# Modulation vectors from turned-over weights, by one fused multiply and sum each, moved into the mixers

## The chip, the core and the metric

The kernel runs on one core of a Trainium2 chip. A core has TensorE (matrix products), VectorE (DVE), ScalarE (ACT), GpSimd (POOL) and SyncE (SP, which here issues nearly all transfers); they run side by side and wait for each other by semaphores. The metric is the device time of one execution in microseconds, lower is better.

## The reference, cut to what matters

A decoder trunk of two layers over x (512 positions by 1024 channels). Each layer has three sub-layers, SwiGLU, mixer, SwiGLU, and each of these is scaled and shifted by vectors that are computed from one conditioning vector c:

```python
cs = silu(c)                                             # (1, 1024)
mod = (cs @ ada_w[l] + ada_b[l]).reshape(1, 3, 3, 1024)  # ada_w[l]: 1024 x 9216
h = rmsnorm(x, norm_g[l, s]) * (1 + mod[s, 1]) + mod[s, 0]
x = x + (0.5 if s != 1 else 1) * mod[s, 2] * sublayer(h)
```

So there are 2 x 3 x 3 = 18 modulation vectors of 1024 elements, named (l, s, j) below: layer, sub-layer, and j = 0 shift, 1 scale, 2 gate. Each is a product of a vector of 1024 with a 1024 x 1024 block of `ada_w`, 4 MB of f32 weights.

## The kernel before, in words

Activations stay in SBUF turned over: `xT` holds 128 channels by 512 positions in each of 8 chunks. Every large product is done three times in fp32r with operands split in a high and a low part: `hi = cast(w)` on ACT, `lo = w - hi` on DVE (`Unit.split`, L214 and L215; `sub`, L146), then hi·xh, hi·xl, lo·xh on TensorE (`step`, L235 to L237). The SwiGLU halves (called FFN here) do most of their up projections by a seven-product scheme (`Sums`, `product`, `seven`, L585 and L558), which adds DVE work before each product. A sub-layer ends in `finish`, and `boundary` makes the next norm and the first products of the next sub-layer.

Work beside the main line is written as generators. `tick()` is called after every second `step` (six matmuls) and after each chunk in `values_turned` (twelve matmuls of 256 columns); it adds `rate * share` to a due count and runs one `next` of the current modulation generator for each whole unit. `share` is 0.5 in the up part of an FFN and 2.2 in its down part, and in a mixer the 2.2 of the FFN before it still holds. A gate that a `down` needs and that is not ready is finished there in one go (`while sub_layer not in ready`).

`modulation(l, s, j)` reads the 4 MB as 16 tiles of 128 x 512 (contraction on the partitions), four in flight (`AHEAD`). Each tile is multiplied by a per-partition scalar of `cs` and added to an accumulator on DVE (`weighted`, L309 and L311). After 8 tiles `partition_sums` adds over the partitions: DVE transpose (L316) and reduce (L318), four POOL copies (L322), a DVE reduce (L324), four POOL copies (L327). `modulation_end` adds the bias (L300), then for j = 1 also L303. One vector is 22 `next`s. Sixteen vectors are made so: four in the first FFN, two in the first mixer, four in the second FFN, three in the third, two in the second mixer, one in the last FFN.

The first two vectors, (0,0,1) and (0,0,0), are made in the opening. `ada_load(k)` brings the columns of chunk k, `prepare(k)` runs eight DVE multiply-adds of 128 x 256 (L1266, L311), one add (L1270), two small matmuls with `ones` (L1273), the ends, then t = xT * rms (L1278), hh and u on ACT (L1279, L1280), and hl on POOL (L1281). TensorE multiplies six units chunk by chunk (L1308). The rms of the first norm is a chain of POOL instructions for each of the four row blocks (`rstd_of`, L367 to L372).

F is a pool of 19 tiles of 128 x 512 f32 that all of this shares; a tile that is taken again has to wait for its last reader. Loads into F and into `raw` (four buffers for weights) go through the one SP queue in its order. The framework orders the instructions of each engine by its own estimate of when they are ready, near the order of the program but not equal to it; once ordered, an engine works in order.

In `up()` of an FFN, `begin(m)` starts the seven products of the pair m, m+1: it loads the weights of the pair and does the first product. In the first FFN of layer 0 three units m = 0, 1, 2 are already done in the opening (`first`), and `begin(2)` runs at m = 1 although unit 2 is in `first`; what it starts there is not used.

Of the kernel before, what the change touches and what calls it, by code (L numbers as in the profile page):

```python
# [30 lines left out]
P = 128  # L31
D = 1024
# [15 lines left out]
AHEAD = 4  # L48
CONV_STEPS = (4, 8)
RATE_FIRST, RATE_FFN, RATE_MIX = 0.8, 0.4, 0.2  # L50
# [66 lines left out]
def trunk(ctx: ExitStack, tc: tile.TileContext, x, c, ada_w, ada_b, norm_g, ffn_w_gate, ffn_w_up, ffn_w_down,  # L117
# [152 lines left out]
    vec = const.tile([P, 2 * 72 + 112], F32, name="vec")  # L270
    V_C, V_N, V_CW, V_F = 144, 152, 200, 248
# [24 lines left out]
    def modulation_end(l, s, j, dst, src, k):  # L296

        n = dst.shape[1]
        b = l * 72 + s * 24 + j * 8 + k
        V.tensor_tensor(dst, src, vec[:, b:b + n], op=ALU.add)  # L300
        if j == 1:
            g = V_N + l * 24 + s * 8 + k
            V.scalar_tensor_tensor(dst, dst, 1.0, vec[:, g:g + n], op0=ALU.add, op1=ALU.mult)  # L303
        elif j == 2 and s != 1:
            V.tensor_scalar(dst, dst, 0.5, None, op0=ALU.mult)

    def weighted(acc, w, k):
        if k == 0:
            V.tensor_scalar(acc, w, cs[:, 0:1], None, op0=ALU.mult)  # L309
        else:  # L310
            V.scalar_tensor_tensor(acc, w, cs[:, k:k + 1], acc, op0=ALU.mult, op1=ALU.add)  # L311

    def partition_sums(acc):

        flat = F.take()
        V.transpose(flat.ap, acc)  # L316
        part = sp.tile([P, 16], F32, tag="part", bufs=2, name="part")
        V.tensor_reduce(part, flat.ap.rearrange("p (j i) -> p j i", i=32), op=ALU.add, axis=AX.X)  # L318
        flat.give()
        four = sp.tile([32, 4, 16], F32, tag="four", bufs=2, name="four")  # L320
        for a in range(4):
            G.tensor_copy(four[:, a], part[32 * a:32 * a + 32])  # L322
        one = sp.tile([32, 16], F32, tag="one", bufs=2, name="one")
        V.tensor_reduce(one, four.rearrange("p a j -> p j a"), op=ALU.add, axis=AX.X)  # L324
        dot = sp.tile([P, 4], F32, tag="dot", bufs=2, name="dot")
        for a in range(4):
            G.tensor_copy(dot[32 * a:32 * a + 32], one.rearrange("p (k a) -> p a k", a=4)[:, a])  # L327
        return dot

    def modulation(l, s, j):  # L330

        m = mod(l, s, j)
        ahead = []

        def fetch(n):
            if n < 2 * NC:
                w = F.take()
                col = s * 3 * D + j * D + n // NC * S
                nc.sync.dma_start(w.ap, ada_w[l, n % NC * P:(n % NC + 1) * P, col:col + S])
                ahead.append(w)  # L340

        for n in range(AHEAD):
            fetch(n)
        for half in range(2):
            acc_slot = F.take()
            acc = acc_slot.ap
            for k in range(NC):
                w = ahead.pop(0)
                weighted(acc, w.ap, k)
                w.give()  # L350
                fetch(half * NC + k + AHEAD)
                yield
            yield
            dot = partition_sums(acc)
            acc_slot.give()
            yield
            modulation_end(l, s, j, m[:, 4 * half:4 * half + 4], dot, 4 * half)
            if half:
                ready.add((l, s, j))
            yield  # L360


    def rstd_of(st, n, eng=V):

        w = sp.tile([P, 4, 4], F32, tag="rs", bufs=3, name="rs")
        ms, q, e = (w[:, k, :n] for k in range(3))
        eng.tensor_scalar(ms, st, 1.0 / D, EPS, op0=ALU.mult, op1=ALU.add)  # L367
        G.tensor_tensor(q, ms, minus_half[:, :n], op=ALU.pow)
        G.tensor_tensor(e, q, q, op=ALU.mult)
        G.tensor_tensor(e, e, ms, op=ALU.mult)  # L370
        G.tensor_scalar(e, e, -0.5, 1.5, op0=ALU.mult, op1=ALU.add)
        G.tensor_tensor(q, q, e, op=ALU.mult)  # L372
        return q
# [271 lines left out]
    def ffn(l, i, get, first, whole):  # L645
# [45 lines left out]
        def up(part):  # L691
            modulating["share"] = SHARE_UP
            for m in range(*part):
                if m in acts:
                    continue
                if m < len(first) or m % 2:
# [8 lines left out]
                    if m % 2:  # L705
                        begin(m + 1)
# [484 lines left out]
    for r in range(2):  # L1191
        nc.sync.dma_start(xin[r].ap, x_rows[r])
    c_rows = rows([c.rearrange("b (k p) -> (b k) p", p=P), norm_g.rearrange("l s (k p) -> (l s k) p", p=P),
          conv_w.rearrange("l t (k p) -> (l t k) p", p=P), final_g.rearrange("(k p) -> k p", p=P)], V_C)
# [3 lines left out]
    cs = const.tile([P, NC], F32, name="cs")  # L1198
# [3 lines left out]
    def ada_load(k):  # L1202
        s = F.take(4)
        v = s.ap.rearrange("p (k m) -> p k m", k=NC)
        for j in range(2):
            col = (1 - j) * D + k * P
            nc.sync.dma_start(v[:, :, j * P:(j + 1) * P],
                              ada_w[0][:, col:col + P].rearrange("(k p) m -> p k m", p=P))
# [20 lines left out]
    q = []  # L1229
    for r in range(4):  # L1230
        A.activation(hl[:, 0:2].rearrange("p a b -> p (a b)"), xin[r].ap, AF.Square, accum_out=ssq[:, r:r + 1])
        q.append(rstd_of(ssq[:, r:r + 1], 1, G))
# [10 lines left out]
        if r == 1:  # L1243
            c_rows()
            A.activation(cs, vec[:, V_C:V_C + NC], AF.Silu)
            b_rows()
    rb = bank("at")
    for r in range(4):
        T.transpose(rb[:, r * P:(r + 1) * P], q[r].to_broadcast([P, P]), ident)
# [3 lines left out]
    ada_load(2)  # L1253
# [156 lines left out]
```

## Time and profile before

| | us |
|---|---|
| median of 3 runs (2702.79 to 2708.17) | 2703.82 |
| the profiled execution | 2702.54 |
| its span, first to last instruction | 2700.7 |
| PE busy | 2632.2 (97%) |
| DVE busy | 1898.2 (70%) |
| ACT busy | 1167.8 (43%) |
| POOL busy | 311.2 (12%) |
| DMA, mean over the span | 121 GB/s |

The mean granted TensorE clock is 0.991 of full speed. Busy time of PE is not PE at its peak, since matmuls overlap; what shows that PE waits is idle time between its instructions. The shares are means over stages that differ, so the rows below go by stage.

### The profile page before, as it was taken

What the parts mean: (1) busy time and instruction counts of PE and PEld (TensorE: products, weight loads), DVE (VectorE), ACT (ScalarE), POOL (GpSimd) and SP (SyncE); (2) the same over time, 40 slices, a digit from 0 to 9 for tenths busy, and PEclk for the clock granted to TensorE, in tenths of its full rate; (3) what the DMA queues carried; (4) which work ended last, traced back from release to release, by engine and by line L of the source; (5) the groups of instructions that cost most, each with busy time, mean ns of one, the idle gap of its engine ahead of it and who ended that gap; (6) DMA issues with size and microseconds to landing.
All of it is one profiled execution on the core that took longest, in us unless ns stands there. A gap on an engine that the chain in (4) does not pass through costs nothing.

```text
span 2700.7 us, 41538 instructions
## 1 busy us (share of the span) xinstructions
PE 2632.2 (97%) x16321; PEld 2357.8 (87%) x16321; DVE 1898.2 (70%) x2987; ACT 1167.8 (43%) x2202; POOL 311.2 (12%) x887
## 2 busy tenths in 40 slices
PE   6899999999999999999999999999999999999998
PEld 5788999888888889899998999988888888989998
DVE  7997878665463349997788987767646534787666
ACT  4433454443453235344554544543443423535443
POOL 3110103110010001100021000321110000200001
PEclk8999999999999999999999999999999999999999
DMA  8644435432222233563335541534322322342321
GB/s 251 222 158 149 131 123 161 129 94 82 82 82 91 86 117 108 189 198 100 109 107 192 171 127 61 180 110 137 98 56 87 124 75 90 106 129 89 115 69 73
DMA packets 320209, 328.08 MB, mean 121 GB/s; under 512 B 10130, under 2 KB 283917, under 8 KB 320013
## 3 DMA queue, kind: packets, MB, share of 16 engines
q1 hardware_dynamic: 319684, 325.29, 38.0%
q8 instruction: 128, 2.10, 0.3%
q14 instruction: 69, 0.56, 0.1%
q10 hardware_dynamic: 328, 0.13, 0.0%
HBM read 323.25 MB, written 2.13 MB: 120 GB/s over the span
## 4 chain that ended last, share of the span: by engine, by line
PE 76%; DVE 12%; ACT 4%; DMA 3%; issue 2%; POOL 2%; ACTq 0%; SPq 0%; DVEq 0%; POOLq 0%
PE mm L235 12%; PE mm L236 12%; PE mm L558 12%; PE mm L237 12%; PE o L558 6%; DVE slots_r L146 4%; PE mm L1073 3%; PE at L558 3%; PE o L235 2%; PE o L237 2%; PE o L236 2%; DVE slots_f L311 2%; DMA raw<-in_ffn_w_down_dram 2%; PE at L237 2%; PE at L235 2%
## 5 line engine op out<-in xcount | busy, mean ns | idle before, releaser
L215 DVE TENSOR_TENSOR slots_r<-raw,slots_r 128x512 fp32r<-128x512 f32 (+2 forms) x578 | 360.2, 641 | 299.4 <-PE mm L236 155.0
L214 ACT CAST slots_r<-raw 128x512 fp32r<-128x512 f32 (+1 forms) x584 | 323.4, 582 | 411.3 <-PE mm L237 157.3
L237 PE MATMUL mm<-hh,slots_r 128*128 128x512 f32 (+1 forms) x1320 | 482.8, 366 | 7.5 <-DVE slots_r L215 7.5
L235 PE MATMUL mm<-hh,slots_r 128*128 128x512 f32 (+1 forms) x1320 | 487.8, 370 | 0.0
L236 PE MATMUL mm<-hl,slots_r 128*128 128x512 f32 (+1 forms) x1320 | 483.5, 366 | 0.0
L146 DVE TENSOR_TENSOR slots_r<-raw,slots_r 128x1024 fp32r<-128x1024 f32 (+3 forms) x402 | 379.5, 969 | 90.2 <-ACT slots_r L549 32.6
L549 ACT CAST slots_r<-raw 128x1024 fp32r<-128x1024 f32 x274 | 283.4, 1048 | 351.6 <-DVE raw L585 146.9
L237 PEld LDWEIGHTS mm<-hh,slots_r 128*128 128x128 f32 x1320 | 248.8, 188 | 51.1 <-DVE slots_r L215 7.8
L235 PEld LDWEIGHTS mm<-hh,slots_r 128*128 128x128 f32 x1320 | 249.1, 189 | 36.9
L236 PEld LDWEIGHTS mm<-hl,slots_r 128*128 128x128 f32 x1320 | 249.2, 189 | 36.2
L558 PE MATMUL mm<-slots_r 128*128 128x256 f32 x1872 | 240.8, 284 | 6.9 <-ACT slots_r L549 5.8
L558 PE MATMUL mm<-hh,slots_r 128*128 128x256 f32 x1264 | 236.7, 283 | 9.1 <-ACT slots_f L581 6.6
L558 PE MATMUL o<-slots_r 128*128 128x256 f32 x1872 | 236.4, 284 | 5.2 <-DVE slots_r L146 3.1
L558 PEld LDWEIGHTS mm<-slots_r 128*128 128x128 f32 x1872 | 230.9, 192 | 9.8 <-ACT slots_r L549 6.8
L558 PEld LDWEIGHTS o<-slots_r 128*128 128x128 f32 x1872 | 229.9, 191 | 8.4 <-DVE slots_r L146 4.2
L236 PE MATMUL mm<-slots_r 128*128 128x512 f32 (+1 forms) x584 | 213.1, 365 | 1.2 <-DVE slots_r L146 1.2
L235 PE MATMUL mm<-slots_r 128*128 128x512 f32 (+1 forms) x584 | 212.7, 364 | 0.6 <-ACT slots_r L676 0.6
L237 PE MATMUL mm<-slots_r 128*128 128x512 f32 (+1 forms) x584 | 212.2, 363 | 0.0
L558 PEld LDWEIGHTS mm<-hh,slots_r 128*128 128x128 f32 x1264 | 199.1, 190 | 12.7 <-ACT slots_f L581 9.5
L311 DVE SCALAR_TENSOR_TENSOR slots_f<-slots_f,cs 128x512 f32<-128x512 f32 (+1 forms) x272 | 192.2, 721 | 12.0 <-DMA slots_f<-in_ada_w_dram 11.1
L585 DVE TENSOR_TENSOR raw<-raw 128x1024 f32<-128x1024 f32 x156 | 189.6, 1217 | 1.4
L558 PE MATMUL mm<-hl,slots_r 128*128 128x256 f32 x632 | 177.7, 281 | 0.0
(207 smaller groups left out, 4518.7 us busy)
## 6 DMA issues: line engine op xcount, KB each, us to landing
slots_f<-in_ada_w_dram SPq DMA_DIRECT2D x256, 256.0 KB, 2.9
raw<-in_w_in_dram SPq DMA_DIRECT2D x52, 1024.0 KB, 5.1
raw<-in_ffn_w_gate_dram SPq DMA_DIRECT2D x43, 1024.0 KB, 5.2
raw<-in_ffn_w_up_dram SPq DMA_DIRECT2D x43, 1024.0 KB, 5.3
raw<-in_ffn_w_down_dram SPq DMA_DIRECT2D x32, 768.0 KB, 5.8
raw<-in_w_in_dram SPq DMA_DIRECT2D x48, 512.0 KB, 5.2
raw<-in_ffn_w_down_dram SPq DMA_DIRECT2D x20, 512.0 KB, 3.6
slots_f<-in_ada_w_dram SPq DMA_DIRECT2D x16, 512.0 KB, 7.5
```

What stands on the lines that cost most here:

```text
L146: V.tensor_tensor(out_, a, b, op=ALU.subtract)
L214: A.copy(hv, src)
L215: (eng or V).tensor_tensor(lv, src, f(hv), op=ALU.subtract)
L235: T.matmul(dst, hi, xh[:, cols], start=first, stop=False)
L236: T.matmul(dst, hi, xl[:, cols], start=False, stop=False)
L237: T.matmul(dst, lo, xh[:, cols], start=False, stop=last)
L311: V.scalar_tensor_tensor(acc, w, cs[:, k:k + 1], acc, op0=ALU.mult, op1=ALU.add)
L549: A.copy(hv, src)
L558: T.matmul(dst, a, b, start=first and k == i == n == 0, stop=True, skip_group_check=True)
L585: V.tensor_tensor(dst, x, y, op=ALU.subtract)
L1073: T.matmul(dst, a, b, start=k == 0 and r % 2 == 0 and n == 0, stop=True, skip_group_check=True)
```

## The change

- The weights arrive turned over (`ada_t`: 9216 x 1024 for each layer), so the contraction runs along the free axis. `cs` becomes a tile of 128 x 1024, the vector repeated on all partitions by a transfer and Silu applied there; it holds two tiles of F to the end.
- `weighted` is one DVE instruction (`tensor_tensor_reduce`) over 128 x 1024 f32: multiply by `cs`, sum along the row, one output element on each partition. A vector takes 8 of them, 8 loads of 512 KB, one end, 9 `next`s. `partition_sums` goes.
- In the opening `prepare(k)` runs two of these in place of the nine instructions and the matmuls with `ones`; t of chunk 0 and all of hl move from POOL to DVE. The four rms chains become one over 4 columns, after the last row block.
- `rstd_of` keeps `pow` on POOL and does the rest on DVE, three instructions in place of four, also at every boundary.
- The FFNs make no modulation vectors but for three in the first one. The first mixer makes ten: (0,1,2), (0,2,1), (0,2,0), (0,2,2), three of (1,0,·), three of (1,1,·); the second mixer three. The rate there is 0.28 in place of 0.2, and one load is in flight (`depth=1`) in place of four.
- `begin(m + 1)` is not called where unit m + 1 is in `first`.

```diff
-AHEAD = 4
-RATE_FIRST, RATE_FFN, RATE_MIX = 0.8, 0.4, 0.2
+RATE_FIRST, RATE_FFN, RATE_MIX = 0.6, 0.3, 0.28
...
-    def weighted(acc, w, k):
-        if k == 0:
-            V.tensor_scalar(acc, w, cs[:, 0:1], None, op0=ALU.mult)
-        else:
-            V.scalar_tensor_tensor(acc, w, cs[:, k:k + 1], acc, op0=ALU.mult, op1=ALU.add)
+    def weighted(m, k, w):
+        V.tensor_tensor_reduce(out=w, in0=w, in1=cs.ap, scale=1.0, scalar=0.0, op0=ALU.mult, op1=ALU.add,
+                               accum_out=m[:, k:k + 1])
...
-    def modulation(l, s, j):
+    def modulation(l, s, j, depth=2):
         m = mod(l, s, j)
         ahead = []
-        def fetch(n):
-            if n < 2 * NC:
-                w = F.take()
+        def fetch(k):
+            if k < NC:
+                w = F.take(2)
+                nc.sync.dma_start(w.ap, ada_rows(l, s, j, k))
                 ahead.append(w)
+        for k in range(depth):
+            fetch(k)
+        for k in range(NC):
+            w = ahead.pop(0)
+            weighted(m, k, w.ap)
+            w.give()
+            fetch(k + depth)
             yield
+        modulation_end(l, s, j, slice(0, NC))
+        ready.add((l, s, j))
+        yield
...
         G.tensor_tensor(q, ms, minus_half[:, :n], op=ALU.pow)
-        G.tensor_tensor(e, q, q, op=ALU.mult)
-        G.tensor_tensor(e, e, ms, op=ALU.mult)
-        G.tensor_scalar(e, e, -0.5, 1.5, op0=ALU.mult, op1=ALU.add)
-        G.tensor_tensor(q, q, e, op=ALU.mult)
+        V.tensor_tensor(e, q, q, op=ALU.mult)
+        V.scalar_tensor_tensor(e, e, -0.5, ms, op0=ALU.mult, op1=ALU.mult)
+        V.scalar_tensor_tensor(q, e, 1.5, q, op0=ALU.add, op1=ALU.mult)
...
-                    if m % 2:
+                    if m % 2 and m + 1 >= len(first):
                         begin(m + 1)
...
+    cs = F.take(2)
+    nc.scalar.dma_start(cs.ap, c.to_broadcast([P, D]))
+    A.activation(cs.ap, cs.ap, AF.Silu)
...
+    q = rstd_of(ssq, 4)
...
     def prepare(k):
         s, v = ada_in.pop(k)
+        for j in range(2):
+            weighted(mod(0, 0, j), k, v[:, j])
+            modulation_end(0, 0, j, slice(k, k + 1))
         s.give()
         t, u = F.take(), F.take()
-        (V if k else G).tensor_tensor(t.ap, xT[:, k], rbs.ap, op=ALU.mult)
+        V.tensor_tensor(t.ap, xT[:, k], rbs.ap, op=ALU.mult)
...
-        G.tensor_tensor(hl[:, k], u.ap, f(hh[:, k]), op=ALU.subtract)
+        sub(hl[:, k], u.ap, f(hh[:, k]))
...
+        if l == 0:
+            modulate((RATE_FIRST, modulation(0, 0, 2)),
+                     *((RATE_FFN, g) for g in (modulation(0, 1, 1), modulation(0, 1, 0), bias_rows())))
+        else:
+            modulate()
...
+        ahead = [(l, 1, 2), (l, 2, 1), (l, 2, 0), (l, 2, 2)]
+        if l + 1 < DEPTH:
+            ahead += [(l + 1, s, j) for s in range(2) for j in (1, 0, 2)]
+        modulate(*((RATE_MIX, modulation(*a, depth=1)) for a in ahead if a not in ready))
```

## Rows read from the trace of the kernel before

**Rows 1.** Busy time by stretch: stretch, length, each engine, clock, DMA share, GB/s.
```profile
0.00:79.00 79.00, 54.73 (x218) 42.60 (x219) 58.41 (x123) 31.64 (x52) 30.35 (x47) 0.85 0.88 255
92.00:400.00 308.00, 302.45 (x2023) 277.31 (x2022) 263.73 (x371) 129.54 (x200) 29.22 (x70) 0.99 0.47 151
...
448.00:690.00 242.00, 241.29 (x1344) 208.37 (x1343) 151.43 (x269) 102.86 (x273) 42.59 (x182) 1.00 0.35 105
...
1042.00:1343.00 301.00, 291.84 (x2049) 272.92 (x2050) 263.14 (x351) 133.54 (x190) 20.79 (x64) 0.99 0.44 141
...
1400.00:1700.00 300.00, 296.86 (x2116) 279.13 (x2115) 256.05 (x332) 136.82 (x199) 14.04 (x48) 1.00 0.43 139
...
1760.00:1830.00 70.00, 70.00 (x442) 62.61 (x441) 45.59 (x81) 31.60 (x86) 14.33 (x64) 1.00 0.39 113
...
2350.00:2650.00 300.00, 295.01 (x2082) 276.49 (x2080) 227.42 (x276) 137.32 (x192) 3.70 (x16) 0.99 0.31 101
```

**Rows 2.** Busy time by stretches of 50 us, the same columns.
```profile
1100.00:1150.00 50.00, 46.80 (x285) 41.76 (x284) 47.53 (x70) 17.42 (x24) 4.87 (x19) 1.00 0.48 156
...
1500.00:1550.00 50.00, 50.00 (x398) 48.96 (x397) 46.55 (x63) 26.45 (x42) 2.86 (x8) 1.00 0.54 175
```

**Rows 3.** PE in order of time: start, us, line; idle before it and its releaser.
```profile
91.40 0.80 PE L237 MATMUL mm<-hh,slots_r 128*128 128x512 f32 x1 [7.55 <-DVE slots_r L215]
```

**Rows 4.** Groups of DVE instructions by form: busy us, mean ns, idle before.
```profile
L215 DVE TENSOR_TENSOR slots_r<-raw,slots_r 128x512 fp32r<-128x512 f32 x466 | 314.6, 689 | 277.0 <-PE mm L236 153.5 <-PE o L236 42.9 <-issue 33.0
L585 DVE TENSOR_TENSOR raw<-raw 128x1024 f32<-128x1024 f32 x156 | 189.6, 1217 | 1.4
L311 DVE SCALAR_TENSOR_TENSOR slots_f<-slots_f,cs 128x512 f32<-128x512 f32 x224 | 168.1, 755 | 12.0 <-DMA slots_f<-in_ada_w_dram 11.1
...
L316 DVE STREAM_TRANSPOSE slots_f<-slots_f 128x512 f32<-128x512 f32 x32 | 22.5, 703 | 0.1
...
L318 DVE TENSOR_REDUCE part<-slots_f 128x16 f32<-128x512 f32 x32 | 21.6, 676 | 0.2
...
L309 DVE TENSOR_SCALAR slots_f<-slots_f,cs 128x512 f32<-128x512 f32 x32 | 15.4, 480 | 0.9 <-DMA slots_f<-in_ada_w_dram 0.9
...
L300 DVE TENSOR_TENSOR mod<-dot,vec 128x4 f32<-128x4 f32 x32 | 5.2, 162 | 22.0 <-POOL dot L327 21.9
...
L1322 DVE TENSOR_TENSOR slots_f<-hh,hl 128x2048 f32<-128x2048 f32 x2 | 4.6, 2284 | 1.2 <-POOL hl L1281 1.2
```

**Rows 5.** DVE in order of time: the first instruction on weights of `ada_w`.
```profile
13.43 0.61 DVE L1266 TENSOR_SCALAR slots_f<-slots_f,cs 128x256 f32<-128x256 f32 x2 [2.99 <-DMA slots_f<-in_ada_w_dram]
```

**Rows 6.** ACT in order of time: the first and the last hh of the opening.
```profile
24.34 0.81 ACT L1279 ACTIVATE hh<-slots_f,mod,mod 128x512 fp32r<-128x512 f32 x1 [3.58 <-DVE mod L303]
...
73.55 0.82 ACT L1279 ACTIVATE hh<-slots_f,mod,mod 128x512 fp32r<-128x512 f32 x1 [5.24 <-DVE mod L303]
```

**Rows 7.** Busy time by stretch in the opening, columns as in the first group.
```profile
4.50:7.50 3.00, 2.37 (x11) 2.40 (x12) 0.69 (x1) 2.25 (x4) 0.19 (x1) 1.00 1.01 372
10.00:13.00 3.00, 1.54 (x7) 1.54 (x8) 0.44 (x1) 2.39 (x6) 1.82 (x9) 0.74 1.17 306
30.00:50.00 20.00, 13.73 (x52) 10.02 (x52) 17.61 (x40) 6.25 (x10) 5.92 (x4) 0.89 0.80 207
```

**Rows 8.** Groups of PE instructions from 78.9 to 81.7 us.
```profile
L558 PE MATMUL mm<-hh,slots_r 128*128 128x256 f32 x16 | 2.9, 276 | 0.0
L558 PE MATMUL mm<-hl,slots_r 128*128 128x256 f32 x8 | 2.2, 276 | 0.0
```

**Rows 9.** First mixer, matmuls of L237 alone: PE, PEld, clock, DMA share, GB/s.
```profile
448.00:690.00 242.00, 92.39 (x235) 44.06 (x234) 1.00 0.35 105
```

**Rows 10.** First mixer, matmuls of L1073 alone, the same columns.
```profile
448.00:690.00 242.00, 42.21 (x356) 42.05 (x357) 1.00 0.35 105
```

**Rows 11.** Who waited for the weights of `ada_w`: engine, tile, line: us, times.
```profile
  DVE slots_f L311: 11.1, 12
```

**Rows 12.** Transfers issued in the first 110 us: count, KB each, us to landing.
```profile
slots_f<-in_x_dram SPq DMA_DIRECT2D x4, 512.0 KB, 5.1
```

## The prediction before the run

> **What bounds the kernel now.** I read the busy time by stretch first, with cuts at the stages. TensorE is idle for next to nothing in the mixers: 0.7 us of 242 in the first one. It loses time in two kinds of place. The opening has 24.3 us of idle PE in 79, and its granted clock is at 0.85. The four FFNs have 5.5, 9.2, 3.1 and 5.0 us, 22.8 in all [rows 1]. The DVE column of the same rows is the reason to look at: 264 of 308, 263 of 301, 256 of 300 and 227 of 300 us in the FFNs against 151 of 242 in the mixer. The finer cut shows that the share alone does not fix the loss: at 47.5 of 50 us PE lost 3.2, at 46.6 of 50 nothing [rows 2]. The largest single gap stands right behind the opening: 7.55 us until a DVE split at 91.40 [rows 3]. So this kernel is bound by TensorE, and by DVE in the opening and in the FFNs. A change pays where it takes DVE work out of those, and costs where it puts it somewhere that becomes as full.
>
> **What a vector costs.** Now, on DVE: 14 multiply-adds of 0.755 us, 2 multiplies of 0.480 and for each half 0.703 + 0.676 + 0.162, together 14.6 us, and 22.0 us of waiting for POOL over 16 vectors, 1.4 each; 16 us [rows 4]. A few shorter instructions are left out. The fused instruction over 1024 elements is not in this trace. Its nearest row is the subtraction of two f32 tiles of 128 x 1024, 1.217 us; nothing speaks for less, since the 512-element form takes 0.689 and the time grows with the elements. Above, the bound is two passes, for which the 128 x 2048 row stands, 2.284 us. I take 1.25, by the near row and a little for writing the sum: a vector is then 8 x 1.25 + 2 x 0.16 = 10.3 us [rows 4].
>
> The multiply-add of today also reads two f32 tiles from SBUF (the weights and the accumulator) and takes 0.755 us for 512 elements, near the 0.689 of a plain two-tile operation and far from 1.2 [rows 4]. [...]
>
> **The opening.** Per chunk DVE gets 2 x 1.25 for the sums, three ends of 0.16, t and hl at 0.69 each: 4.36 us, 34.9 for eight chunks, and six splits of 0.69 stay on it: 39 us [rows 4]. The first weights are used at 13.43 [rows 5]; the repeated `cs` is 0.5 MB more, 1.4 us at 372 GB/s, and the weights come in long rows, as x does, at up to 372 in place of 306, 0.6 us less for the first MB [rows 7]: 14.2. Without gaps the last hh would come at 53; with DVE busy for 88% of the time, as it is from 30 to 50 us [rows 7], at 58.5. It comes at 73.55 now, 49.2 us behind the first one, 7.0 per chunk [rows 6]. The first hh no longer waits for four POOL chains and a product with `ones`, but eight chunks in series set the end and not the first one. That is 15 to 20 us, and I take 17. The lower bound is the transfer: x, `cs`, eight MB of `ada_w` and four MB of weights are 15.2 MB, which at the 255 GB/s of the whole opening [rows 1] land at 63, so that the last hh comes at 66: 7.5 us. The upper bound is 22, with less contention than now. POOL loses hl and most of the rms and gains nothing.
>
> What follows the last hh up to 91.40 is DVE work of the FFN that stays, so the 7.55 gap moves and does not shrink. The unused product is 24 matmuls in 2.7 us [rows 8], but they lie ahead of that gap; PE would have waited there. Its saving is the split of 1.2 us on DVE: 1 us.
>
> **The FFNs.** The first keeps three vectors of 10.3 in place of four of 16: 33 us less of 264. The second loses 64 us of DVE work, the third 48, the last 16, all of theirs. Some idle stays at the start of each, where the sums for the seven products fill DVE in any case. I keep 1.5 to 2 us each: gains of 4, 7, 1.5 and 3 of the idle in [rows 1], 15.5 in all. Bounds: 6, if the gaps hang on the sums, and 22, all idle.
>
> **The mixers** pay. Ticks in the first stretch: 235 / 2 + 356 / 12 = 147 in 242 us, one every 1.65 us [rows 9, 10]. Ten vectors are 90 `next`s at 0.28 x 2.2 = 0.616 a tick, 146 ticks, 240 us: the same stretch. Its DVE work is 151 us, some 25 of it the vectors of today; 126 + 103 = 229 of 242, 95% [rows 1]. The second mixer makes three in 44 ticks, 72 us: 46 - 11 + 31 = 66 of 70 [rows 1]. At such shares PE lost 0 to 3.2 us in 50 [rows 2], so 0 to 20 us over 314. I take 7, nearer the lower end, because in a mixer the splits run ahead of PE.
>
> **The waits added** are those of `pow` at every boundary: DVE starts it, POOL computes, DVE goes on. Behind the waiting instruction stand the residual updates, for which the norm and the next products wait. Three DVE instructions of 0.16 replace four POOL ones, and each side keeps its hand-overs; 0, within 2 either way. Fewer SP issues (128 in place of 256 for the 16 vectors) are worth nothing by themselves, since SP is not what PE waits for.
>
> **Sum** against the profiled execution of 2702.5 (span 2700.7 and 1.8 around it): -17 - 1 - 15.5 + 7 = -26.5, so 2676. The median of the runs lies 1.3 above that execution: 2677.
>
> **Rivals.**
>
> *The opening is held by its transfers.* It gains 7.5, and the FFNs keep the gaps of their first sums, so 9.5; the mixers cost 7. 2704 - 10 = 2694. For it: DMA is at 0.88 over the whole opening [rows 1]. Against: the mean includes waits for free tiles, and from 30 to 50 us DMA is less busy than DVE [rows 7].
>
> *The single load in flight takes the gain back.* This is the one on the slower side. With `depth=1` the next 512 KB are asked for when the sum before is queued, often into the tiles just freed, while up to eight logits and other tiles fill F. A load that starts only then holds DVE for its landing, 5.1 us [rows 12], and everything on SP's queue behind it, `raw` loads included. DVE has 13 us to spare in the first mixer. It decides when 13 + 33.5 us are used up, that is 46 / 5.1 = 9 of the 80 loads fully exposed; with 12, the time is 2704 + 15 = 2719. For it: F is short of pairs in the mixers and DVE is near full. Against: DVE waited only 12 times, 11.1 us in all, for 256 such loads [rows 11].
>
> *The fused sum runs at half rate*, 2.28 us [rows 4]. A vector costs 18.6: 126 + 186 = 312 us of DVE in 242, 70 over; 35 + 56 = 91 in 70, 21 over; the opening gains nothing; the FFNs 14. 2704 + 77 = 2781. [...]
>
> **How the numbers follow.** My forecast has 65%, its own range 2660 to 2692. Held transfers 18%, the single load 12%, the half rate 5%. A measurement of this kernel can tell about 0.2%, 5.4 us, from no change. Held transfers: 15 of the 18 lie below 2698.4, 3 within. The single load: 9 of 12 slower, 3 within. So faster 80%, same 6%, slower 14%. The range goes from 2656 (the opening at its bound of 22, the FFNs at 22, the mixers at 0, less a little) to 2704, which leaves out the slower cases and a few per cent below.
>
> **What would show it.** Right: the fused sum at 1.2 to 1.3 us; the last hh of the opening near 56 us and the long PE gap near 74; idle PE in the second FFN down to 2 us; DVE at 93% or more in the first 240 us of the first mixer, and PE idle there a few us more than 0.7. Wrong: a last hh later than 66 (transfers); DVE idle for `ada_t` in the mixers for more than 20 us, with PE gaps behind it (single load); a fused sum over 2 us; or FFNs whose gaps stay with DVE under 70%, which would mean that the vectors were never their cause.

## The result, and the profile after

Four runs of the changed kernel took 2683.68 to 2692.47 us, median 2686.59; the kernel before, run beside it, 2703.31. The ratio is 0.9937, with a 95% interval of 0.9916 to 0.9958: faster by 0.6%. The profiled execution of after took 2685.69 us, with a span of 2683.9, so the working below compares 2683.9 with the 2700.7 of before.

The busy time of after in the same stretches (stretch, length, then busy time and count of each engine, granted clock, DMA share, GB/s) answers to [rows 1]:

```profile
0.00:79.00 79.00, 52.52 (x213) 41.79 (x213) 59.88 (x107) 39.05 (x60) 10.59 (x15) 0.87 0.75 260
92.00:400.00 308.00, 307.32 (x2141) 285.39 (x2140) 247.23 (x349) 142.94 (x229) 13.30 (x20) 1.00 0.42 137
448.00:690.00 242.00, 231.68 (x1288) 198.54 (x1287) 192.54 (x358) 98.56 (x266) 49.17 (x134) 0.99 0.69 226
1042.00:1343.00 301.00, 296.61 (x2067) 276.35 (x2068) 219.19 (x269) 138.15 (x208) 0.00 (x0) 1.00 0.31 102
1400.00:1700.00 300.00, 299.14 (x2091) 280.36 (x2092) 221.63 (x275) 136.83 (x207) 3.12 (x6) 1.00 0.33 106
...
2350.00:2650.00 300.00, 297.68 (x2073) 278.69 (x2074) 217.74 (x271) 133.07 (x200) 0.00 (x0) 0.99 0.29 95
```

VectorE left the FFNs: 263 us of 301 became 219 in the second. In these cuts TensorE's idle time fell there from 9.2 to 4.4 us, in the first FFN from 5.5 to 0.7, in the third from 3.1 to 0.9. In the first mixer VectorE went up only from 151 to 193 of 242 us, 80%, and yet TensorE lost 10.3 us where it had lost 0.7.

The fixed cuts shift against the stages when a kernel gets faster, so a part of such a fall can be a gap that now lies outside the cut. Better marks are the 12 matmuls with `ones` at the start of each boundary's norm. In after (TensorE in order of time: start, us, line):

```profile
386.49 1.40 PE L396 MATMUL at<-ones,slots_f 128*128 128x1 f32 x12
1000.88 1.40 PE L396 MATMUL at<-ones,slots_f 128*128 128x1 f32 x12
1358.19 1.40 PE L396 MATMUL at<-ones,slots_f 128*128 128x1 f32 x12
1709.74 1.40 PE L396 MATMUL at<-ones,slots_f 128*128 128x1 f32 x12
2308.34 1.40 PE L396 MATMUL at<-ones,slots_f 128*128 128x1 f32 x12
2664.30 1.40 PE L396 MATMUL at<-ones,slots_f 128*128 128x1 f32 x12
```

The differences are the stages (boundary included); the same marks give them for every kernel of this study, each from its own profiled execution. Among the kernels made from after, a stage that an edit leaves alone agrees within 2 to 3 us in most cases; the first mixer and the second FFN differ by up to 4 or 5, so smaller differences in those two are not read as effects. A part of such differences goes with TensorE's granted clock, which is not constant: its mean was 1.00 from 476 to 485 us of after and 0.60 from 485 to 489. The second FFN from mark to mark, in before, in after and in e2, which edits only the mixers (columns as above):

```profile
1010.01:1371.31 361.30, 352.06 (x2502) 330.14 (x2501) 309.37 (x448) 167.21 (x261) 37.03 (x92) 1.00 0.45 143
...
1000.88:1358.19 357.31, 350.78 (x2503) 328.92 (x2501) 261.00 (x352) 168.32 (x261) 14.23 (x20) 1.00 0.30 98
...
990.71:1353.45 362.74, 355.54 (x2503) 333.35 (x2501) 261.51 (x352) 168.53 (x261) 14.36 (x20) 0.99 0.30 96
```

Against after, e2 has 0.7 us more idle time of TensorE there and 4.8 us more busy time for the same 2503 matmuls, at a mean clock of 0.99 in place of 1.00.

| kernel | opening + FFN 1 | mixer 1 | FFN 2 | FFN 3 | mixer 2 | FFN 4 | end | span |
|---|---|---|---|---|---|---|---|---|
| before | 409.7 | 600.3 | 361.3 | 351.9 | 600.9 | 356.4 | 20.2 | 2700.7 |
| after | 386.5 | 614.4 | 357.3 | 351.6 | 598.6 | 356.0 | 19.6 | 2683.9 |
| e3, short sums | 384.9 | 614.7 | 359.1 | 351.9 | 599.2 | 354.7 | 19.5 | 2684.0 |
| e9, one load of eight | 387.8 | 598.8 | 359.1 | 351.6 | 599.0 | 356.2 | 19.4 | 2672.0 |
| e1, two loads | 387.8 | 609.6 | 358.8 | 350.6 | 598.6 | 353.8 | 19.3 | 2678.5 |
| e2, slow pace | 387.3 | 603.4 | 362.7 | 351.0 | 599.3 | 356.1 | 19.3 | 2679.2 |
| e7, two and slow | 386.0 | 604.0 | 357.5 | 350.7 | 598.5 | 353.7 | 19.4 | 2669.8 |
| e12, slower still | 386.5 | 602.7 | 358.9 | 350.8 | 597.3 | 354.8 | 19.4 | 2670.4 |
| e5, sums in the FFNs | 387.5 | 598.3 | 364.5 | 351.8 | 599.7 | 357.5 | 19.4 | 2678.6 |
| e8, GpSimd's queue | 386.5 | 651.2 | 357.4 | 351.6 | 610.0 | 357.6 | 20.5 | 2734.7 |
| e4, product restored | 389.8 | 617.4 | 357.6 | 351.9 | 598.6 | 357.0 | 21.0 | 2693.3 |
| e10, before without it | 401.9 | 599.3 | 369.1 | 355.5 | 599.7 | 355.0 | 19.7 | 2700.2 |
| e6, rms on GpSimd | 387.7 | 611.0 | 359.6 | 352.8 | 602.6 | 356.3 | 19.8 | 2689.7 |
| e11, splits to VectorE | 383.5 | 618.4 | 360.0 | 352.9 | 599.3 | 356.2 | 19.3 | 2689.7 |

From before to after: opening and first FFN 23.2 gained, first mixer 14.1 lost, second FFN 4.0 gained, second mixer 2.3, the rest 1.4 together. That is 16.8, the difference of the spans.

The fused sum, as a group over the whole run (busy us, mean ns, idle before and its releaser), with the instruction that reads its result out:

```profile
L297 DVE CUSTOM_DVE_ANT_0 slots_f<-slots_f 128x1024 f32<-128x1024 f32 x144 | 176.1, 1232 | 42.0 <-DMA slots_f<-in_ada_t_dram 41.0 <-POOL slots_r L967 0.4
L297 DVE DVE_READ_ACCUMULATOR2_ANT mod<- 128x1 f32 x144 | 11.5, 80 | 0.0
```

A vector costs 8 x 1.31 = 10.5 us and one or two short ends; 10.3 was forecast with the ends. The multiply-adds had waited 11 us for their loads [rows 11], the sums wait 41.

In the opening, ScalarE's first and last hh answer to [rows 6]:

```profile
26.91 0.81 ACT L1239 ACTIVATE hh<-slots_f,mod,mod 128x512 fp32r<-128x512 f32 x1 [1.55 <-DVE slots_f L1238]
...
62.23 0.81 ACT L1239 ACTIVATE hh<-slots_f,mod,mod 128x512 fp32r<-128x512 f32 x1 [3.24 <-DVE mod L305]
```

and TensorE's gap behind the opening answers to [rows 3]:

```profile
81.20 0.79 PE L236 MATMUL at<-hh,slots_r 128*128 128x512 f32 x1 [6.78 <-DVE slots_r L214]
```

The first hh is 2.6 us later than before, the last 11.3 sooner, and the gap ends 10.2 sooner.

Now the first mixer, from mark to mark, in before and in after:

```profile
409.72:1010.01 600.29, 597.67 (x3183) 511.39 (x3182) 335.06 (x602) 245.49 (x572) 74.87 (x266) 1.00 0.33 102
...
386.49:1000.88 614.39, 602.20 (x3182) 512.12 (x3181) 397.77 (x732) 244.52 (x570) 86.42 (x229) 1.00 0.47 154
```

Of the 14.1 us, 9.6 are idle time of TensorE (12.2 for 2.6) and 4.5 are longer busy time for the same matmuls. In 386 to 696 us, what VectorE waited for (us in total, times, longest):

```profile
DVE slots_f L297 <- DMA slots_f<-in_ada_t_dram: 27.7, 20, 3.4
```

and SyncE's queue:

```profile
SPq L321 <- DVE mod L297: 126.1, 49, 6.0
SPq L193 <- DVE slots_r L214: 42.8, 14, 9.9
```

In the 49 waits of the first line, a load has to go into a pair of tiles that a fused sum still reads, in most cases the sum two or three before the one that the load is for. So it is asked for only when that sum is done, and the loads issued from 448 to 690 us land a median 4.6 us later. One place where this reaches TensorE, on VectorE in order of time:

```profile
473.21 1.23 DVE L297 CUSTOM_DVE_ANT_0 slots_f<-slots_f 128x1024 f32<-128x1024 f32 x1 [2.71 <-DMA slots_f<-in_ada_t_dram]
...
475.93 1.23 DVE L297 CUSTOM_DVE_ANT_0 slots_f<-slots_f 128x1024 f32<-128x1024 f32 x1 [1.49 <-DMA slots_f<-in_ada_t_dram]
...
483.53 1.23 DVE L297 CUSTOM_DVE_ANT_0 slots_f<-slots_f 128x1024 f32<-128x1024 f32 x1 [1.68 <-DMA slots_f<-in_ada_t_dram]
...
485.36 0.68 DVE L145 TENSOR_TENSOR slots_r<-at,slots_r 128x512 fp32r<-128x512 f32 x1
```

and on TensorE:

```profile
480.68 0.40 PE L236 MATMUL mm<-hh,slots_r 128*128 128x512 f32 x1
...
486.10 1.44 PE L884 MATMUL o<-slots_r 128*128 128x256 f32 x5 [4.47 <-DVE slots_r L145]
487.33 0.63 PE L234 MATMUL mm<-hh,slots_r 128*128 128x512 f32 x1
```

The split of the attention weights at 485.36 is what TensorE needs. Three sums stand ahead of it in VectorE's order, and they waited 5.9 us for loads within 14 us. VectorE is not full here: it is held in its order. Behind the gap TensorE also works more slowly for a while: the 128x512 matmul takes 0.63 us in place of 0.40, and the mean granted clock from 485 to 489 us is 0.60.

### The profile page after: what moved, and what is told of

The parts are those of the page before. It is cut to its first block, busy times and chain, and to the rows that moved or that the text cites. A ratio compares the mean times of both kernels' runs of the same rounds, so it can differ in the third digit from the quotient of the medians.

```text
span 2683.9 us, 40526 instructions
## 1 busy us (share of the span) xinstructions
PE 2620.5 (98%) x16265; PEld 2347.2 (87%) x16265; DVE 1838.3 (68%) x2874; ACT 1171.6 (44%) x2200; POOL 227.7 (8%) x551
## 4 chain that ended last, share of the span: by engine, by line
PE 84%; DVE 9%; DMA 3%; ACT 3%; issue 1%; POOL 1%; DVEq 0%; POOLq 0%; SPq 0%; ACTq 0%
PE mm L531 16%; PE mm L234 12%; PE mm L235 12%; PE mm L236 12%; PE o L531 8%; PE at L531 4%; PE mm L1046 3%; DMA slots_f<-in_ada_t_dram 2%; DVE slots_f L297 2%; PE o L234 2%; PE o L236 2%; PE o L235 2%; PE at L236 2%; PE at L234 2%; PE at L235 2%; DVE slots_r L145 2%
## 5 line engine op out<-in xcount | busy, mean ns | idle before, releaser
L213 ACT CAST slots_r<-raw 128x512 fp32r<-128x512 f32 (+2 forms) x584 | 325.1, 582 | 403.2 <-PE mm L236 170.9
L531 PE MATMUL mm<-hh,slots_r 128*128 128x256 f32 x1248 | 229.5, 280 | 2.7 <-DVE slots_r L145 1.3
L297 DVE CUSTOM_DVE_ANT_0 slots_f<-slots_f 128x1024 f32<-128x1024 f32 x144 | 176.1, 1232 | 42.0 <-DMA slots_f<-in_ada_t_dram 41.0
```

The source lines that it names most:

```text
L213: A.copy(hv, src)
L297: V.tensor_tensor_reduce(out=w, in0=w, in1=cs.ap, scale=1.0, scalar=0.0, op0=ALU.mult, op1=ALU.add, accum_out=m[:, k:k + 1])
L531: T.matmul(dst, a, b, start=first and k == i == n == 0, stop=True, skip_group_check=True)
```

## The experiments

**What costs the first mixer its 14 us: VectorE's share, or the late loads?** The forecast had priced the share. Two kernels separate them.

*e3* keeps all loads and cuts the sums; *e9* keeps all sums and cuts the loads.

```
e3:  def weighted(m, k, w, n=D): ... in0=w[:, :n], in1=cs.ap[:, :n]
     -  weighted(m, k, w.ap)
     +  weighted(m, k, w.ap, P)
e9:  -  if k < NC:            # fetch
     +  if k < loads:         # 1 in the mixers
     +  if k >= loads - 1 and k < NC - 1: ahead.append(w)   # sum the same piece again
```

> The changed kernel in which the vectors made beside the FFN and the mixers sum only 128 of their 1024 products; the loads are the same, so this leaves out most of the DVE work and none of the transfers (the sums are not the reference's). Theory B (DVE share): the stretch of the first mixer falls from 614.4 to 602, the time to about 2673. Theory A (late loads): DVE still waits for the weights, more than before since it comes sooner to each; the stretch stays above 609 and the time above 2680.

> The complement of the short sums: in the mixers each of the ten vectors loads only the first of its eight pieces and sums that one eight times at full width, so 7/8 of the mixers' modulation loads are left out while VectorE's work stays. Theory (the late loads hold VectorE in its order, its share of work does not matter): the first mixer's stretch falls from 614.4 to 598 to 602 us with VectorE as busy as in the changed kernel (about 400 us of it), waits for ada_t there fall from 27.7 us to under 6, and the time is 2670 to 2675. Rival (the 98 us of sums there are the cost): the stretch stays at 611 to 615 and the time at 2683 to 2687.

e3: 2686.53 us, ratio 0.9947 (0.9934 to 0.9959), first mixer 614.7. From 388 to 988 us VectorE was busy 321 us in place of 391, and nothing was gained; its waits for loads, 386 to 696, became

```profile
DVE slots_f L297 <- DMA slots_f<-in_ada_t_dram: 76.0, 51, 3.9
```

e9: 2674.27 us, ratio 0.9893 (0.9879 to 0.9906). The waits of the same stretch, and 388 to 988 us as one window:

```profile
DVE slots_f L297 <- DMA slots_f<-in_ada_t_dram: 0.8, 1, 0.8
```

```profile
388.00:988.00 600.00, 598.24 (x3192) 512.33 (x3192) 397.40 (x733) 244.92 (x571) 87.64 (x229) 1.00 0.31 97
```

VectorE is as busy as in after (397 us against 391) and TensorE loses 1.8 us of 600. The mixer takes 598.8, no more than before the change. The 80 sums, 105 us of VectorE work (the mixer's VectorE time is 62 us above that of before), cost nothing there; the loads cost 15.6 (614.4 less 598.8). They did not do it by slowing VectorE's own instructions, whose busy time is the same in both kernels. The short sums show it from the other side: VectorE with more free time only waited more.

**More loads in flight, and a slower pace.** e1 lets two loads run ahead (with one more f32 tile, 20 in place of 19); e2 lowers the pace of the mixers' sums; e7 does both; e12 lowers the pace once more.

```
e1:  -  modulation(*a, depth=1)     +  modulation(*a, depth=2)     N_F 19 -> 20
e2:  -  RATE_MIX = 0.28             +  RATE_MIX = 0.16
e7:  both                           e12: both, RATE_MIX = 0.1
```

> The changed kernel with two loads of modulation weights in flight in the mixers in place of one, and 20 tiles in F in place of 19. Theory A (DVE stands still for weights that are asked for too late, into tiles just freed: 22.9 us of DVE waits in the first mixer): the waits fall under 8 us, the stretch from the norm before the first mixer to the norm after it falls from 614.4 to about 606, and the time from 2686.6 to about 2679. Theory B (the 100 us of DVE work added to the first mixer cost PE its time, whenever the weights come): the stretch stays within 2 us of 614, the time within 3 us of 2686.6.

> The changed kernel with a rate of 0.16 in place of 0.28 in the mixers, so that the ten vectors of the first one spread over some 256 ticks (420 us) in place of 146 (240 us). Theory B (DVE share): DVE in the first 240 us of the mixer falls from 0.83 to about 0.70, the stretch of the mixer from 614.4 to about 603, the time to about 2676. Theory A (late loads): a sum every 4.7 us leaves a load of 4.5 us just enough time; waits fall by half, stretch about 608, time about 2681. If the bytes themselves were the cost (transfers of the mixer weights held up), the same bytes in more time: stretch about 603 as well, with the raw loads landing sooner.

> The changed kernel with both: two loads in flight in the mixers (20 tiles in F) and a rate of 0.16. Late loads (now the theory: with the sums cut to an eighth the first mixer kept all of its cost) says that the two mend the same wait, so that together they leave little of it: DVE waits for these weights under 10 us in the first mixer (27.7 in the changed kernel, 30.7 with the slow rate alone), the stretch from norm to norm at 601 to 603 (600.3 before the change, 614.4 changed, 603.4 slow rate, 609.6 two loads), the time about 2673. Rival: what is left at the slow rate is DVE share or ordering and not waits: waits fall but the stretch stays at 603 to 605 and the time at 2675 to 2678.

> The version with two loads ahead and the slower pace (2673.87), with the pace lowered once more from 0.16 to 0.10 of a column's time, so that the ten vectors spread over most of the first mixer instead of its first 310 us. Theory (each wait is a load that was asked for too late beside the mixer's own loads): waits for ada_t in the first 310 us fall from 28 us to under 18, the first mixer's stretch from 604 to 599 to 602, the time to 2668 to 2672. Rival (what is not done by the mixer's end is made up for in one go ahead of the second FFN): the stretch is 605 to 620 and the time 2675 to 2690.

| kernel | median us | ratio to before | first mixer | waits for loads, 386 to 990 | last sum there at |
|---|---|---|---|---|---|
| after | 2686.59 | 0.9937 (0.9916 to 0.9958) | 614.4 | 27.7 | 660 |
| e1 | 2682.31 | 0.9925 (0.9911 to 0.9938) | 609.6 | 17.4 | 661 |
| e2 | 2676.69 | 0.9907 (0.9893 to 0.9920) | 603.4 | 36.6 | 809 |
| e7 | 2673.87 | 0.9889 (0.9875 to 0.9902) | 604.0 | 33.7 | 806 |
| e12 | 2674.23 | 0.9890 (0.9876 to 0.9903) | 602.7 | 56.3 | 966 |

The forecasts of these runs held only in part. e1 came out between its two theories (609.6 us, 17.4 us of waits). e2 met the stage and the time that the theory of VectorE's share gave it (603 and 2676), while its waits rose, where late loads had them halved; what speaks against the share is e3 and e9. e7 met its time, but its waits were to fall under 10 us and did not.

e7 is the fastest version of the whole computation, 12.7 us under the change as it was made, and its interval lies below that of after; e12 is its equal. The pace is worth more than the second load: 11.0 us of the mixer against 4.8, and 4.8 is little more than what that stage differs by anyway. The column of waits does not order the kernels. The slow ones wait longer in total and lose less. A likely reason, which no run tests by itself, is that their waits lie further apart and VectorE makes up for each before TensorE has used what was split ahead. e12 was expected to keep its waits in the first 310 us under 18; they were 23.1, and the time missed its range by 2 us: the still slower pace bought nothing more. In e7, 448 to 690 us:

```profile
448.00:690.00 242.00, 239.96 (x1360) 207.54 (x1359) 169.89 (x310) 104.74 (x277) 43.88 (x134) 1.00 0.54 173
```

TensorE's 10.3 us of idle are down to 2.0.

**Is it SyncE's queue?** e8 takes the mixers' modulation loads out of it.

```
-  nc.sync.dma_start(w.ap, ada_rows(l, s, j, k))
+  queue.dma_start(w.ap, ada_rows(l, s, j, k))      # queue = GpSimd's in the mixers
```

> The changed kernel with the loads of the mixers' modulation weights issued from POOL's queue in place of SP's, still one in flight. It parts two ways in which a late load can cost: (1) DVE stands still in front of the sum and what is queued behind it on DVE comes late to PE; then the queue does not matter, waits on DVE stay at 20 to 35 us, the stretch stays at 612 or more, the time at 2685 or more (POOL's own copies for the attention may come later still). (2) SP stands still in front of the load (164 us there) and the mixer weights behind it come late; then the stretch falls to about 604 and the time to about 2677.

2736.65 us, ratio 1.0118 (1.0105 to 1.0132): slower than before. The first mixer took 651 us. What GpSimd waited for from 386 to 1037 us, and TensorE in the same stretch:

```profile
POOL slots_f L321 <- DVE mod L297: 134.2, 45, 7.8
```

```profile
PE o L884 <- DVE slots_r L145: 18.4, 7, 11.2
PE at L775 <- ACT slots_r L994: 13.8, 4, 6.1
```

The wait for the pair in use moves with the load. Now it holds GpSimd's own work behind it, of which the softmax has a part in every block, and the longest gap of TensorE grows from 4.5 to 11.2 us. VectorE waited 61.0 us for the loads in place of 27.7. SyncE was the better place to wait. Of the 37 us, 27 are more idle time of TensorE and 10 longer busy time, at a mean clock of 0.97 over the stage; how much is GpSimd's blocked work and how much the later loads was not separated.

So e8 does not say what SyncE's own 126 us of waiting cost. The waits of after do. From 386 to 1000 us neither TensorE nor VectorE waits for one of the mixer's own weights that stand behind these loads in SyncE's queue, and ScalarE waits for them once:

```profile
ACT slots_r L213 <- DMA raw<-in_w_conv_out_dram: 2.0, 1, 2.0
```

In before the longest wait of this kind was 2.7 us. The held queue, and the added traffic as far as it could delay the mixer's weights, are therefore not what costs TensorE its time in after.

**Did the move into the mixers pay?** e5 makes the fused sums where the old kernel made its vectors, in the FFNs with two loads ahead.

```
-  modulate((RATE_FIRST, modulation(0, 0, 2)), ...)     # layer 0 only: three vectors in FFN 1, ten in the mixer
+  modulate(*gens, *((RATE_FFN, g) for g in [modulation(l, 1, 1), ..., modulation(l, 1, 2)]))
   ...   # the vectors of the next stages in FFN 1 to 4, two in a mixer, as before the change
```

> The changed kernel with the vectors made where the old kernel makes them (four, two, four, three, two, one), with two loads in flight in the FFNs and the rates of the changed kernel: the fused sum and the new opening without the move into the mixers. From the stretches: the move cost 14 us in the first mixer and gave about 5 in the three later FFNs, so without it the time is about 2679, the first mixer back at 601 to 603, the second FFN at 358 to 361 from norm to norm. Rival (the move pays, DVE in the FFNs is what binds): the FFNs give back 9 us or more and the time is 2688 or more.

2680.36 us, ratio 0.9921 (0.9907 to 0.9934), 6.2 under the changed kernel, though the two intervals overlap. The first mixer is back at 598.3; the second FFN takes 364.5, 7.2 more than in after and above the 358 to 361 expected. So with one load in flight the move cost the mixer at least what it gave the FFNs. With the loads mended (e7) the move pays: 2673.87, and its interval lies below that of e5.

**The unused product.** e4 is the changed kernel with it restored, e10 the kernel before without it.

```
-  if m % 2 and m + 1 >= len(first):        # e4; e10 the other way
+  if m % 2:
```

> The changed kernel with the unused product of the first FFN put back. By the prediction its 24 matmuls fall into the gap ahead of the first split (6.78 us now), so that only its DVE split counts: 1 us, time 2686 to 2689. Rival: its two loads of 1 MB and its casts delay what the gap waits for, and one more F tile is held: the gap ends 4 us later or more, time 2690 or more.

> The kernel before with one edit of the change alone: the unused first product is not started. If it costs its own stretch what the run with it restored lost there (3.3 us up to the first mixer) and the rest of that run's 8 us was a different order in the mixer, the time is 2699 to 2701. If the product is worth 8 us wherever it stands, 2695 to 2696. The prediction's price (only its VectorE split, 1 us): 2702 to 2703.

e4: 2695.08 us, ratio 0.9965 (0.9953 to 0.9978), so 8.5 us over the changed kernel. By stage it loses 3.3 us up to the first mixer, 3.0 in it (not more than such differences), and 2.4 in the last FFN and at the end; nothing was edited behind the first FFN. The 3.3 can be followed. In after the first and the last of 24 matmuls of a needed product, on TensorE in order of time, stand ahead of the gap that ends at 81.20:

```profile
68.30 0.39 PE L234 MATMUL mm<-hh,slots_r 128*128 128x512 f32 x1
...
73.57 0.39 PE L236 MATMUL mm<-hh,slots_r 128*128 128x512 f32 x1
```

In e4 the unused product's 24 small matmuls (16 on hh, 8 on hl) stand there instead, from 67.78 to 70.6 us. The weight split that the needed ones wait for releases TensorE only at 77.53, where in after the last split ahead of them was made at 61.44, so 22 of the 24 come behind the gap:

```profile
77.53 0.80 PE L236 MATMUL mm<-hh,slots_r 128*128 128x512 f32 x1 [5.17 <-DVE slots_r L214]
78.12 0.63 PE L234 MATMUL mm<-hh,slots_r 128*128 128x512 f32 x1
...
84.23 0.40 PE L236 MATMUL mm<-hh,slots_r 128*128 128x512 f32 x1
```

The gap ends 3.7 us sooner, but 7 us of needed matmuls are left behind it; the difference is the 3.3. Up to the first mixer TensorE is idle for 28.7 us in after and 28.8 in e4: the unused matmuls come on top and fill no idle time.

e10: 2708.74, ratio 1.0019 (1.0010 to 1.0028): no gain by itself, rather a small loss, which none of the three prices had. Its profiled execution took 2702.02 us, the lowest of its runs, so the stages below do not show the whole of it. It reaches the first mixer 7.8 us sooner and gives 7.8 back in the second FFN, where VectorE has the same 310 us of work as in before and TensorE is idle for 14.4 us in place of 9.2. TensorE's waits there, 1001 to 1371 us:

```profile
PE mm L558 <- DVE slots_r L146: 8.5, 7, 2.6
PE mm L558 <- ACT slots_r L549: 1.7, 1, 1.7
```

So the edit is worth 3.3 us in its place in the changed kernel. Most of the rest of the 8.5 goes with TensorE's clock. TensorE's busy time in the profiled execution of after and of e4:

```profile
PE 2620.5 (98%) x16265; PEld 2347.2 (87%) x16265; DVE 1838.3 (68%) x2874; ACT 1171.6 (44%) x2200; POOL 227.7 (8%) x551
...
PE 2631.3 (98%) x16289; PEld 2356.9 (88%) x16289; DVE 1839.2 (68%) x2875; ACT 1171.8 (44%) x2202; POOL 233.6 (9%) x551
```

With spans of 2683.9 and 2693.3 us, TensorE is idle for 63.4 and 62.0 us, so no longer in e4; it is busy 10.8 us longer, of which the 24 unused matmuls are 2.8. The mean granted clock is 0.993 in after and 0.989 in e4 (in the other runs 0.992 to 0.993 and 0.990 to 0.991), and 0.004 of 2690 us is 11 us. In the first mixer both kernels run 3182 matmuls, idle for 12.2 and 11.7 us, but busy for 602.2 and 605.7. Why the mean clock was lower in e4, and why e10 gains nothing, stays open.

**The norm's chain.** e6 puts the rest of the rms chain back on GpSimd, as one chain; e11 leaves it on VectorE and gives VectorE the opening's weight splits that ran on GpSimd.

```
e6:   -  V.tensor_tensor(e, q, q, ...)   (three on VectorE)   +  four on G
e11:  -  u.split(0, G)                                        +  u.split(0, V)
```

> The changed kernel with the rms chain back on POOL after the power (four short instructions), still one chain for the four row blocks. In the opening three DVE instructions of 4 elements took 1.19 to 1.22 us each, beside POOL splits. Theory: the first hh comes 2 us sooner (26.9 to about 24.9) and the opening ends 2 us sooner; boundaries within 0.5 us each; time about 2684. Rival: the opening is a series of eight chunks that waits for weights and tiles further on, so an earlier first hh is lost by the fourth: last hh at 62.2 as before, time within 1.5 us of 2686.6.

> The opening's weight splits that GpSimd made (four of 128x512 x1.23 us at 19.9 to 24.8, and the pair behind) go to VectorE. Theory (the three 128x4 operations of the rms chain took 1.19 to 1.22 us because GpSimd's splits held the memory that both read): they fall to under 0.3 us each, the first hh comes at 24 to 25 us instead of 26.9, VectorE takes on about 4 us of splits, the last hh stays within 61 to 64 us and the time within 2684 to 2690. Rival (these small operations take 1.2 us by themselves): they stay at 1.2, the last hh comes at 65 to 67 and the time is 2689 to 2692.

e6: 2691.5 us, ratio 0.9958 (0.9946 to 0.9971). The first hh came at 25.10, 1.8 sooner, the last at 62.63, no sooner: the first hh does not set the opening. The time is above both forecasts: the second mixer lost 4.0 us, 2.4 of them idle time of TensorE, which neither side had said and no run explains.

e11: 2687.72, ratio 0.9941 (0.9929 to 0.9953), the same as after. VectorE's chain in after, beside GpSimd's four splits from 19.85 to 24.77 us:

```profile
19.91 1.22 DVE L343 TENSOR_TENSOR rs<-rs 128x4 f32<-128x4 f32 x1 [0.91 <-POOL rs L342]
...
21.16 1.19 DVE L344 SCALAR_TENSOR_TENSOR rs<-rs 128x4 f32<-128x4 f32 x1
...
22.38 1.19 DVE L345 SCALAR_TENSOR_TENSOR rs<-rs 128x4 f32<-128x4 f32 x1
```

and in e11, with the splits on VectorE itself:

```profile
20.11 0.16 DVE L343 TENSOR_TENSOR rs<-rs 128x4 f32<-128x4 f32 x1 [0.92 <-POOL rs L342]
...
20.80 0.16 DVE L344 SCALAR_TENSOR_TENSOR rs<-rs 128x4 f32<-128x4 f32 x1
...
21.54 0.16 DVE L345 SCALAR_TENSOR_TENSOR rs<-rs 128x4 f32<-128x4 f32 x1
```

The three took 1.2 us because of GpSimd's splits; that the cause is a memory which both read, as the theory has it, no run shows. The last hh came at 57.95 in place of 62.23, sooner than the 61 expected, although VectorE took on six splits, and TensorE's gap ended at 77.00. The first mixer starts 3.0 us sooner and takes 4.0 longer, which is within what that stage differs by; whether the waits for loads there take back an earlier start is not shown.

## Why the prediction was right, and where not

The time of 2677 was 9.6 us too low and inside the range of 2656 to 2704, and the forecast of faster held, because the opening and the first FFN gave more than all else took. Of the 26.5 us forecast 16.8 came: the FFNs 2 to 4 fell short by 6.7 and the mixers by 4.8, the first part gave 1.2 more, and 0.6 at the end was not in the sum. The terms:

*Opening, unused product and first FFN*: -17, -1 and -4, 22 in all. Measured 23.2. The parts were not right. With the product kept (e4) the gap ends 13.9 us sooner, not 17, 3.3 fall to the product, and 6.0 are left for the first FFN. The mechanism of the opening, eight chunks in series on VectorE, is borne out as far as an earlier first hh changed nothing (e6). The last hh lies between the forecast's 58.5 and the 66 of held transfers, and the long gap ended at 81.20, not near 74. What was missed is how slow VectorE's two-tile operations were beside GpSimd's splits (1.79 us for a multiply that took 0.68 elsewhere in after, 2.31 for a sum that took 1.22; with the splits moved, in e11, the last hh came 4.3 us sooner), and that the order put 3.5 us of other VectorE work between the last sum's end at 58.50 and the end of its vector at 62.04: the 2.28 us sum of hh and hl for the seven products, and two splits.

*Unused product*: the failed step is "they lie ahead of that gap; PE would have waited there". They do lie ahead of it, but TensorE does not wait in their place: without them it runs matmuls that otherwise come behind the gap (e4), and that is worth 3.3 us.

*FFNs 2 to 4*: -7, -1.5, -3. Measured -4.0, -0.4, -0.4. In the cuts of [rows 1] idle time did fall by 4.8, 2.3 and 2.7, but these cuts begin 9 to 16 us later in the stages of after and leave out gaps that before had inside them. From mark to mark it went from 9.2 to 6.5, from 3.1 to 2.8 and from 5.3 to 5.1 us. Behind the first 50 us of each FFN it did fall (5.1 to 2.3, 1.8 to 0.0, 1.7 to 0.4), but in these 50 us it grew (4.1 to 4.3, 1.3 to 2.8, 3.6 to 4.7). The step that failed here is "I keep 1.5 to 2 us each": what stays at the start of each is more. The largest single gap of the second FFN is left at its start, where no modulation is made any more (TensorE in order of time):

```profile
1043.75 2.90 PE L531 MATMUL o<-slots_r 128*128 128x256 f32 x22 [3.28 <-DVE slots_r L145]
```

For these three stages and the first together 10.8 were measured, midway between the 15.5 taken and the lower bound of 6, "if the gaps hang on the sums" for the seven products.

*Mixers*: +7. Measured +14.1 and -2.3, so +11.8. This is the step that failed: "At such shares PE lost 0 to 3.2 us in 50". The pace was right (80 sums between 411 and 660 us, 240 us forecast), the work per vector too. But the loss does not hang on the share. From 411 to 661 us in after, and in 250 us from the same point of the work in e9, with one load of eight:

```profile
411.00:661.00 250.00, 238.91 (x1272) 201.71 (x1271) 215.01 (x392) 94.87 (x228) 50.78 (x122) 0.99 0.73 241
...
412.00:662.00 250.00, 249.34 (x1403) 215.88 (x1402) 221.36 (x408) 107.69 (x282) 57.95 (x154) 1.00 0.34 104
```

VectorE stands at 86% where TensorE loses 11.1 us, and at 89% where it loses 0.7. (The 80% of the cut from 448 us is lower because that cut lies 23 us later in the stage than before.) The loss came from the rival's mechanism, the single load in flight, at a smaller size. The rival needed nine loads fully exposed, 46 us; there were 20 waits of 1.4 us, 27.7 in all. Its point of decision was set too high, since it gave VectorE's free time as cover. Free time does not cover a wait in the middle of an order: e3 had 70 us more of it and lost the same 14 us. The sign that the prediction itself named, more than 20 us of idle VectorE for these loads with gaps behind, was there.

*The fused sum at half rate*: did not occur. 1.232 us for 1024 elements stands beside 1.217 for a plain two-tile operation [rows 4].

## What to carry to other kernels

A load that has to wait for a buffer to be released can hold everything behind its consumer, however idle that engine looks (here three sums waited 5.9 us for loads, and TensorE 4.47 us for the split behind them, with VectorE busy for 80% of the time from 448 to 690 us); before moving work onto an engine with free time, count the loads in flight and the buffers that they need, not the busy share. To tell the two apart, cut the compute and keep the loads, then keep the compute and cut the loads. Compare stage lengths and idle time at marks in the work, not at fixed times, and read the granted clock of each stage beside them before a few us are put down to an edit.

## What was not expected of the hardware

Operations of four elements took 1.19 to 1.22 us on VectorE while GpSimd split weights from SBUF (after), and 0.16 us without (e11). Larger ones suffered too: at 38.95 and 40.67 us of after, beside GpSimd's two splits from 38.89 to 41.89, a 128 x 512 multiply took 1.79 us and a fused sum 2.31, against 0.68 and 1.22 elsewhere in the same opening. In before, at 20.36 us, a 128 x 256 add took 1.52 us beside GpSimd's multiply and splits from 19.80 to 24.22, against 0.41 at 28.70. The small operations took about as long as one GpSimd split of after, 4.92 / 4 = 1.23 us.
